# A distance-bias table spread over 128 partitions and recorded ahead of the q/k/v projection, and expert rows fetched by indirect DMA, in a two-block transformer kernel

## The chip, the cores and the metric

The kernel runs on one core of a Trainium2 chip. Its time is the device time of one execution in microseconds (us); the median of three runs stands for a kernel. TensorE (PE) does matrix products, its weight loads (PEld) run beside them; VectorE (DVE), ScalarE (ACT) and GpSimd (POOL) do the rest; SyncE (SP) only issues transfers. Sixteen DMA engines serve all transfers of the core.

## The reference

Two transformer blocks in a row on one sequence of 512 tokens of 1024 values, in float32. Two places of them matter here.

The first block's attention adds to each score a bias that depends only on the distance between query and key and on the head (32 buckets of distance, 8 heads):

```
def shared_bias(dist):
    return rel_bias[t5_bucket(dist)].transpose(2, 0, 1).reshape(G, R, *dist.shape)
...
s = jnp.einsum('bgrqd,bgkd->bgrqk', qc, kw) + shared_bias(dist)
p = masked_softmax(s, mask)
```

The second block ends in a mixture of experts: a router picks 2 of 32 experts for each token, and an expert is a gated pair of 1024x256 products and a 256x1024 product:

```
combine = jnp.sum(jax.nn.one_hot(e_idx, N_EXPERTS) * weights[..., None], axis=1)
for e in range(N_EXPERTS):
    act = jax.nn.silu(hf @ w_gate[e]) * (hf @ w_up[e])
    y = y + combine[:, e:e + 1] * (act @ w_down[e])
```

## The kernel before, in words

Everything lies on one core. Weights stream from DRAM in tiles of 128 partitions x 1024 values (512 KB), tokens are handled in four chunks of 128, and products of float32 are made exact enough by splitting operands into a high part and a rest (names ending in h and l).

**What sets the order.** The functions don't issue instructions: they record them in a plan, with tiles that belong to size classes (tags) of a fixed number of buffers; the class "t4" of 128x1024 tiles has 38, and holds streamed weights as well as kept tiles. `order()` (line 264) then runs a list scheduling: each engine, by a simple model of speeds, always takes the first recorded instruction that is ready, and a load may be taken ahead of its place where its class has a buffer to spare. `issue()` (line 400) issues them all, and so nearly every row of the trace names L409. Each engine runs its own list strictly in order. All ordinary transfers are issued by SP, in one list; when one of them must wait (for a buffer, or for the data that it stores), all behind it wait.

**The bias.** `bias_tables()` (line 830) builds a table R of 8 heads x 640 distances on 8 partitions: two products with a one-hot matrix, subtracted from a row of "far" values. One transfer then writes R to DRAM as `Rd`, 128 copies of each head's row (8 x 128 x 640 values, 2.62 MB), so that a read with a row step of 639 gives each query its shifted row. `bias(r)` (line 850) reads the shifted rows of two heads into tiles `B` (128x512 each) and copies from them on DVE the bias of the compressed keys (`cbias`). `nsa(r)` then makes the scores of those heads: PE (kT,qT), DVE (the row maximum `nst`), ACT (the exponential `P`). In `block1()` (line 1199) the order of recording is `qkv(0)` (queries), `compress_in()`, `qkv(1)` (keys, values), `bias_tables()`, the gates, `compress()`, and then the four rounds of `bias(r)` and `nsa(r)`.

**The experts.** `route_chunk` and `route` (lines 1638, 1681) give logits, the two experts of a token and its place (`place`) among the tokens of each expert. `rest_chunk` (line 1669) and `route_chunk` keep the normalised rows of all 512 tokens on the chip, split in a high part `xh` and a rest `xl` (eight t4 tiles). `experts()` (line 1794) goes over 16 pairs of experts; an expert has 64 slots, a pair fills 128 partitions. For each pair `gather()` (line 1777) compares `place` with the slot numbers on DVE (tile `oh`), and 16 products of 128x512 with `xh` and `xl` pick the rows of the slots; two copies (ACT and DVE) bring them to `X`. Then come 8 transposes (ident,X), 32 matmuls with the gate and up weights into H (8 tiles `wg` of 512 KB per pair), the activation, two transposes, 16 matmuls with the down weights (8 tiles `wd` of 256 KB), the scaling by the tokens' weights into `Y`, and an indirect DMA of POOL that adds the rows of Y to the output (`out_rows`) at the tokens given by `si`. `tables()` (line 1756) makes `si` and the slot weights `wt` behind pair 0. If an expert had more than 64 tokens, further rounds would follow.

Of the kernel before, what the change touches and what calls it, by code (L numbers as in the profile page):

```python
# [47 lines left out]
class View:  # L48
    """A part of a planned tile: a stand-in access pattern, and the steps to it from the whole tile."""
# [45 lines left out]
    def box(self):  # L95
        """partitions, range of elements and, where the tile has rows, range in a row."""
# [31 lines left out]
class Offset:  # L128
    """Row offsets of an indirect DMA."""
# [49 lines left out]
class Plan:  # L179
    """Records the instructions of a program in a plain order, then issues them in an order in which every  # L180
    engine, by a simple model of its speed, always takes the first recorded instruction that is ready.  A tile
    is taken ahead of the plain order only where its tag has a buffer to spare up to its place in it."""
# [24 lines left out]
    @contextmanager  # L207
    def together(self):
        """the instructions of the body, all on one engine, stay in one piece."""
        self.grouped = []  # L210
        yield
        g, self.grouped = self.grouped, None
        self.record([(g[0][0][0][0], [x[0][0][1:5] for x in g], None, None, None, sum(x[0][0][5] for x in g), None, False)],
                    [v for x in g for v in x[1]], [v for x in g for v in x[2]])

    def record(self, alts, writes, reads, load=False):
# [9 lines left out]
        for v in reads:  # L226
# [249 lines left out]
def price(self, eng, meth, args, kw):  # L476
    """Nanoseconds that an instruction holds its engine, roughly."""
# [30 lines left out]
class Net:  # L508
# [68 lines left out]
    def pair4(self, name):  # L577
        """four [128, 512] operands of split products."""
# [9 lines left out]
    def slab(self, src, name="w", scale=None):  # L588
        """[128, 1024] of weights: high part and rest; scale: factors of 512 columns."""
# [13 lines left out]
    def mm3(self, ps, pairs, byk=False):  # L603
        """ps = sum over (lhs hi, lhs lo, rhs hi, rhs lo)."""
# [11 lines left out]
    def rsqrt(self, v, n, scale, out=None):  # L616
        """v -> (v * scale + EPS) ** -0.5 on [p, n], in a new small tile or in out."""
# [25 lines left out]
    def constants(self):  # L643
# [11 lines left out]
        # the table of functions, ahead of the data  # L655
# [12 lines left out]
    def load_rows(self, src, name):  # L668
        """the four chunks of rows."""
# [5 lines left out]
    def norm_rows(self, x):  # L675
        """x * rstd, token major."""
# [8 lines left out]
    def new_hT(self, src=None):  # L685
        """hidden states, transposed and split; src: 32 more columns, multiplied on the way."""
# [62 lines left out]
    def scaled(self, out, ps):  # L749
        """out = ps / rms in the first block, ps in the second."""  # L750
# [36 lines left out]
    def narrow(self):  # L787
        """the 32 more columns, token major: psum [128, (chunk, 32)]."""
# [8 lines left out]
    def gemm_t(self, src, name="gt"):  # L797
        """columns on partitions: psum [128 cols, 512 tokens]."""
# [15 lines left out]
    def gemm_part(self, ps, grp, c, lhs_hi, lhs_lo, ks):  # L814
        """adds the products of k tiles ks to ps."""
# [6 lines left out]
    def gemm_r(self, grp, c, lhs_hi, lhs_lo, byk=False):  # L822
        """tokens on partitions: psum [128 tokens of chunk c, 512 cols]."""
# [6 lines left out]
    def bias_tables(self):  # L830
        nc, I = self.nc, self.I
        oh, R = self.t4("tab0")[:32, 0:640], self.t4("tab1")[:8, 0:640]
        nc.sync.dma_start(oh, I["oh"])
        rb = self.small([32, 8], "rb", bufs=1)
        nc.sync.dma_start(rb, I["rel_bias"])
        nc.sync.dma_start(R, I["far"].to_broadcast([8, 640]))
# [13 lines left out]
    def bias(self, r):  # L850
        """negated bias of the two heads of r, [query of a block, key], and that of the compressed keys."""
# [16 lines left out]
    def qkv(self, grp, acc=None, W=None):  # L868
        """q (grp 0) or the keys and values (grp 1): normalised, transposed; values token major."""
# [121 lines left out]
    def silu2(self, ps, name):  # L991
        """2 * silu of a psum tile."""
# [8 lines left out]
    def split_into(self, hi, lo, src, scale):  # L1001
        """hi + lo = src * scale."""
# [4 lines left out]
    def cmp_attention(self, r):  # L1007
        """weights over the compressed keys, times the gate, transposed: [(chunk % 2, g, key), (chunk // 2, query)]."""
# [73 lines left out]
    def lru_setup(self):  # L1082
# [7 lines left out]
        # softplus(-lambda)  # L1090
# [48 lines left out]
    def conv(self, up, wname, bname, i, nt):  # L1139
        """causal depthwise convolution along the tokens of a [128, 512] tile."""  # L1140
# [9 lines left out]
    def log1p(self, out, y, z, q):  # L1150
        """out = log1p(y) for y in [0, 1]; z, q scratch."""
# [10 lines left out]
    def gate_tile(self, wg, i):  # L1162
        """tanh(x / 2) of one tile of merge gates."""
# [8 lines left out]
    def merge(self, wg, g0, wp, a_hi, a_lo, b_hi, b_lo):  # L1172
        """sigmoid gates over two projections, split for the output product."""
# [82 lines left out]
            # sums over the partitions: four groups of 32 equal rows, 256 columns each  # L1256
# [29 lines left out]
    def conv_silu2(self, idx, i):  # L1286
        """2 * silu(conv(.)) of column tile idx."""
# [10 lines left out]
    def prefix(self, p, tri, ones, v, n):  # L1298
        """sums over the tokens up to each one; v [128, (chunk, n)]."""
# [6 lines left out]
    def mgates(self):  # L1306
        """per token and head: a = i - F, exp(-(F + M)); and the rows of M."""
# [83 lines left out]
    def rope_tables(self):  # L1391
        """cos and sin of position * inv_freq, [128, 4 chunks, 8]."""
# [33 lines left out]
    def qk_diff(self, grp, wname, scale, name):  # L1426
        """rms-normalised, rotated, transposed; one [128 = 2 maps x 64, 512] tile per head."""
# [36 lines left out]
    def diff(self, qT, kT, vd, after):  # L1464
        nc = self.nc
        # lam
# [64 lines left out]
    def block2(self):  # L1531
# [40 lines left out]
        for h in range(2):  # L1572
# [7 lines left out]
            for c in range(NCH):  # L1580
# [7 lines left out]
                if h and c:  # L1588
                    self.rest_chunk(c - 1)

# [1 line left out]
    def route_setup(self):  # L1592
        """router weights with the modulation in them, and what the shift adds to the logits."""
# [27 lines left out]
        # per token: its number, weights over the experts  # L1621
# [11 lines left out]
        self.X, self.XT, self.Y = [self.t4(n, keep=True) for n in ("X", "XT", "Y")]  # L1633
        self.x2T, self.sq2, self.gat = {}, {}, {}
        self.xh = [self.t4(f"xh{c}", dt=F32R, keep=True) for c in range(NCH)]
# [372 lines left out]
```

## Time and profile before

| | |
|---|---|
| runs (us) | 1160.14, 1158.07, 1157.68; median 1158.07 |
| span of the profiled execution | 1157.3 us |
| busy, share of the span | PE 1080.1 us (93%), DVE 653.8 (56%), ACT 405.3 (35%), POOL 189.7 (16%) |
| mean DMA rate | 188 GB/s |
| loads of expert weights | wg 128 x 512 KB, wd 128 x 256 KB |

The profile gives the span alone, from the first to the last instruction; the time that a run reports is 0.8 us above it in the median, and that difference is taken as what lies around the span. A share of busy time is an average over stages with different limits, so each stage is read by itself.

### The profile page before, as it was taken

To read this page: it belongs to the slowest core of one execution; us is meant where nothing else is said; L and a number is where in the kernel's file an instruction comes from. 1 tells how busy PE (TensorE), PEld (TensorE's weight loads), DVE (VectorE), ACT (ScalarE), POOL (GpSimd) and SP (SyncE) were. 2 spreads that over 40 slices of the span, in tenths; PEclk is the share of its full clock that TensorE was granted. 3 is DMA by queue.
4 is the path that set the end of the run, shared out by engine and by line. 5 is a ranking of instruction groups with operands and counts; after the bars stand their busy time and mean duration, and the time that the engine had idled before them with its cause. 6 is when DMAs were issued, how large, how long until landed. Compare 5 with 4: busy or idle time off the path is not lost.

```text
span 1157.3 us, 15019 instructions
## 1 busy us (share of the span) xinstructions
PE 1080.1 (93%) x5414; PEld 757.7 (65%) x5414; DVE 653.8 (56%) x1459; ACT 405.3 (35%) x824; POOL 189.7 (16%) x180
## 2 busy tenths in 40 slices
PE   7994299999999999999999999999999999999995
PEld 6773167777788777777677887788787444444431
DVE  4841288989656474776978786544717322333221
ACT  6320166756222243634663342222325111111120
POOL 2300033200111122420130201100204101111011
PEclk9996599999999999999999999999999999999998
DMA  9635810113443471815044322545966999999981
GB/s 346 227 88 87 247 46 20 37 56 95 131 143 119 163 255 53 296 37 220 10 158 157 129 86 73 178 131 156 354 264 219 349 387 363 371 385 367 389 292 26
DMA packets 74506, 217.22 MB, mean 188 GB/s; under 512 B 10820, under 2 KB 12428, under 8 KB 74424
## 3 DMA queue, kind: packets, MB, share of 16 engines
q1 hardware_dynamic: 72120, 211.98, 52.5%
q0 software_dynamic: 2304, 4.20, 2.1%
q8 instruction: 45, 0.74, 0.3%
q14 instruction: 37, 0.30, 0.1%
HBM read 204.56 MB, written 15.22 MB: 190 GB/s over the span
## 4 chain that ended last, share of the span: by engine, by line
PE 60%; DMA 14%; issue 11%; DVE 9%; SPq 2%; ACT 2%; another core or an unknown queue 1%; POOL 0%; POOLq 0%; DVEq 0%; ACTq 0%
PE b L409 59%; DMA out_rows<-Y,si 11%; SPq L409 2%; PE H L409 1%; DVE P L409 1%; DVE dP L409 1%; DMA gr<-in_wo 1%; DMA gr<-in_wa 1%; DMA B<-Rd 1%; DVE ada_acc L409 1%; ACT grh L409 1%; DVE grl L409 1%; DVE dq L409 0%; DVE uc L409 0%
## 5 line engine op out<-in xcount | busy, mean ns | idle before, releaser
L409 PE MATMUL b<-hTh,gth 128*128 128x512 f32 x464 | 124.5, 404 | 0.0
L409 PE MATMUL b<-hTh,gtl 128*128 128x512 f32 x464 | 121.1, 399 | 0.0
L409 PE MATMUL b<-hTl,gth 128*128 128x512 f32 x464 | 119.3, 395 | 0.0
L409 PE MATMUL H<-wg,XT 128*64 128x512 f32 x512 | 114.8, 596 | 0.0
L409 PEld LDWEIGHTS b<-hTh,gth 128*128 128x128 f32 x464 | 86.8, 190 | 22.2 <-issue 3.5
L409 PEld LDWEIGHTS b<-hTh,gtl 128*128 128x128 f32 x464 | 87.0, 189 | 20.5 <-issue 1.6
L409 PEld LDWEIGHTS b<-hTl,gth 128*128 128x128 f32 x464 | 86.4, 188 | 19.4 <-issue 0.9
L409 POOL TENSOR_TENSOR gtl<-gt,gth 128x1024 fp32r<-128x1024 f32 x23 | 56.4, 2455 | 247.0 <-ACT gth L409 222.4
L409 PEld LDWEIGHTS H<-wg,XT 128*64 128x64 f32 x512 | 35.0, 137 | 68.5 <-issue 59.5
L409 DVE SCALAR_TENSOR_TENSOR ada_acc<-ada_w,cols,ada_acc 128x1024 f32<-128x1024 f32 x42 | 60.3, 1435 | 7.5 <-DMA ada_w<-in_w_ada 7.5
L409 POOL DMA_INDIRECT out_rows<-Y,si x16 | 25.0, 1563 | 236.0 <-DVE Y L409 203.0
L409 PE MATMUL b<-grh,hTh 128*128 128x512 f32 x192 | 57.1, 410 | 6.0 <-ACT grh L409 6.0
L409 PE MATMUL b<-kT,qT 64*128 64x128 f32 (+3 forms) x128 | 26.4, 515 | 36.0 <-DVE nst L409 35.9
L409 PE MATMUL b<-wd,aT 128*64 128x512 f32 x256 | 58.4, 598 | 1.5 <-ACT aT L409 1.5
L409 ACT ACTIVATE gth<-gt 128x1024 fp32r<-128x1024 f32 x54 | 56.4, 1049 | 6.7 <-DMA gt<-in_wb 6.6
L409 DVE SCALAR_TENSOR_TENSOR act<-act,H 128x256 f32<-128x256 f32 x32 | 13.4, 420 | 79.6 <-ACT act L409 79.1
L409 PE MATMUL b<-grl,hTh 128*128 128x512 f32 x192 | 57.0, 405 | 0.0
L409 POOL TENSOR_TENSOR grl<-gr,grh 128x1024 fp32r<-128x1024 f32 x15 | 39.4, 2635 | 100.0 <-ACT grh L409 87.6
L409 ACT ACTIVATE P<-P,nst 128x128 f32<-128x128 f32 (+3 forms) x64 | 35.3, 553 | 57.2 <-DVE nst L409 57.0
L409 PE MATMUL b<-grh,hTl 128*128 128x512 f32 x192 | 55.3, 400 | 0.0
L409 DVE SCALAR_TENSOR_TENSOR Y<-b,wt,gate 128x512 f32<-128x512 f32 x32 | 24.0, 750 | 49.8 <-PE b L409 49.4
L409 DVE TENSOR_TENSOR gtl<-gt,gth 128x1024 fp32r<-128x1024 f32 x35 | 42.6, 1222 | 14.8 <-ACT gth L409 13.1
(380 smaller groups left out, 1973.6 us busy)
## 6 DMA issues: line engine op xcount, KB each, us to landing
wg<-in_wgu SPq DMA_DIRECT2D x128, 512.0 KB
wd<-in_wd SPq DMA_DIRECT2D x128, 256.0 KB
gt<-in_wb SPq DMA_DIRECT2D x58, 512.0 KB
ada_w<-in_w_ada SPq DMA_DIRECT2D x48, 512.0 KB
gr<-in_wa SPq DMA_DIRECT2D x23, 512.0 KB
wp<-in_wp SPq DMA_DIRECT2D x16, 512.0 KB
gr<-in_wo SPq DMA_DIRECT2D x16, 512.0 KB
cw<-in_cmp_w SPq DMA_DIRECT2D x8, 512.0 KB
```

The costliest lines, as they stand in the source:

```text
L409: i = getattr(getattr(self.nc, eng), meth)(*[val(a) for a in args], **{k: val(v) for k, v in kw.items()})
```

## The change

**The bias table.** The 32x8 table is spread on chip to 32x128 (each head 16 times), so that one product with the one-hot matrix gives the table on 128 partitions, 16 equal ones for each head; POOL writes the constant of the last 128 columns, and the input "far" goes. `Rd` has the same contents and the same bytes, but is now written from 128 partitions, each of which gives 8 copies. `bias_tables()` is recorded ahead of `qkv(0)`.

**The experts.** `route_chunk` stores the normalised rows of each chunk, unsplit, in a DRAM tile `x2d` (512x1024, 2.1 MB in all). `route` now also makes the slot numbers as it goes (`sl`, and products of `sl` with the token numbers in `slp`), and `slots()` turns them into `si` before pair 0. `fetch(i)` is an indirect DMA of POOL that reads the 128 rows of pair i from `x2d` straight into one of two buffers X; `fetch(0)` stands ahead of the loop and `fetch(i + 1)` at the top of pair i. `rest_chunk`, `gather`, the tiles `xh` and `xl` and the two copies to X are gone; `weights()` takes over the making of `wt`. The rest of the pairs is as before. The diff also drops comments.

```diff
 def bias_tables(self):
-        oh, R = self.t4("tab0")[:32, 0:640], self.t4("tab1")[:8, 0:640]
+        oh, R = self.t4("tab0")[:32, 0:512], self.t4("tab1")[:, 0:640]
...
-        for a, b in ((0, 512), (512, 640)):
-            p = self.pst()
-            nc.tensor.matmul(p[:8, :b - a], rb, oh[:, a:b], start=True, stop=True)
-            nc.vector.scalar_tensor_tensor(R[:, a:b], p[:8, :b - a], -1.0, R[:, a:b], op0=OP.mult, op1=OP.add)
+        rx = self.sq128("rx")[:32, :]
+        nc.vector.tensor_copy(rx.rearrange("p (h i) -> p h i", i=16), rb.unsqueeze(2).to_broadcast([32, 8, 16]))
+        p = self.pst()
+        nc.tensor.matmul(p, rx, oh, start=True, stop=True)
+        nc.gpsimd.memset(R[:, 512:640], BIG)
+        nc.vector.tensor_scalar(R[:, 0:512], p, -1.0, None, op0=OP.mult)
...
-        nc.sync.dma_start(Rd, R.unsqueeze(1).to_broadcast([8, 128, 640]))
+        nc.sync.dma_start(Rd.rearrange("h (i r) m -> (h i) r m", r=8), R.unsqueeze(1).to_broadcast([128, 8, 640]))
...
 def block1(self):
-        self.qkv(0, self.hT_first())
+        acc = self.hT_first()
+        self.bias_tables()
+        self.qkv(0, acc)
         self.compress_in()
         self.qkv(1, W=self.group(I["wa1"][1]))
-        self.bias_tables()
...
 def route_chunk(self, c, h, x):
-        nc.scalar.activation(self.xh[c], x, AF.Copy, scale=r)
+        xn = self.t4("x2n")
+        nc.scalar.activation(xn, x, AF.Copy, scale=r)
+        nc.sync.dma_start(self.x2d[c * 128:(c + 1) * 128, :], xn)
...
 def route(self, lo, hi):
+        for c in range(lo, hi):
+            nc.vector.tensor_tensor(self.sl[:, c].rearrange("p k (a b) -> p k a b", a=2),
+                                    self.io.unsqueeze(1).unsqueeze(1).to_broadcast([128, 2, 2, 64]),
+                                    self.pos[:, c].unsqueeze(2).unsqueeze(3).to_broadcast([128, 2, 2, 64]), op=OP.is_equal)
+            for k in range(2):
+                nc.tensor.matmul(self.slp[:, :32], self.sl[:, c, k], self.tw[:, c, k, 0:32], start=c + k == 0,
+                                 stop=c == NCH - 1 and k == 1)
...
+    def fetch(self, i):
+        self.nc.gpsimd.indirect_dma_start(out=self.X[i % 2], out_offset=None, in_=self.x2d,
+                                          in_offset=Offset(self.si[:, i:i + 1]), bounds_check=511, oob_is_err=False)
...
 def experts(self, first=False):
+        self.fetch(0)
         for i in range(16):
-            ps = self.gather(i, NCH - 1 if first and i < 2 else 0)
-            nc.scalar.activation(X[:, :512], ps[0], AF.Copy)
-            nc.vector.tensor_copy(X[:, 512:], ps[1])
+            X = self.X[i % 2]
+            if i < 15:
+                self.fetch(i + 1)
```

The planner moves instructions on every engine. Three places follow, in rows of each engine's list (destination, sources, size; the numbers behind a name are those of the tile).

SP's list in the first block, where the table is written. Before, behind the weights of the gates (gt) and of the modulation (ada_w):

```order
L409 DMA gt<-in_wb 128x1024 x2
L409 DMA ada_w<-in_w_ada 128x1024
L409 DMA gt<-in_wb 128x1024
L409 DMA Rd<-tab_276 1024x1x640
L409 DMA gt<-in_wb 128x1024
L409 DMA ada_w<-in_w_ada 128x1024
L409 DMA gt<-in_wb 128x1024 x2
L409 DMA ada_w<-in_w_ada 128x1024
L409 DMA gt<-in_wb 128x1024 x2
L409 DMA B_766<-Rd 128x512
L409 DMA B_779<-Rd 128x512
```

With the change, among the weights of the compression (cw) and the stores that shift its keys (kcS):

```order
L409 DMA wd<-in_wd 128x512
L409 DMA cw_335<-in_cmp_w 128x1024
L409 DMA cw_355<-in_cmp_w 128x1024
L409 DMA wd<-in_wd 128x512
L409 DMA Rd<-tab_78 1024x1x640
L409 DMA cw_406<-in_cmp_w 128x1024
L409 DMA kcS<-kcT 64x512 x2
L409 DMA cw_440<-in_cmp_w 128x1024
L409 DMA cw_469<-in_cmp_w 128x1024
L409 DMA kcS<-kcT 64x512 x2
L409 DMA B_518<-Rd 128x512
L409 DMA B_533<-Rd 128x512
```

The write moved from row 41 of SP's list to row 30, and the first reads from row 47 to row 36; the loads of gt that stood between them now stand behind the reads.

PE's list in two consecutive pairs of experts. Before, the 16 products of a gather are mixed among the matmuls of the pair ahead:

```order
L409 MATMUL b<-ident,X 128x128 x8
L409 MATMUL b<-xh_7313,oh 128x512 x2
L409 MATMUL H<-wg,XT 64x512 x16
L409 MATMUL b<-xl_7332,oh 128x512 x2
L409 MATMUL b<-xh_7372,oh 128x512 x2
L409 MATMUL b<-xl_7425,oh 128x512 x2
L409 MATMUL b<-xh_7470,oh 128x512 x2
L409 MATMUL b<-ident,act 128x128 x2
L409 MATMUL b<-xl_7497,oh 128x512 x2
L409 MATMUL b<-xh_7265,oh 128x512 x2
L409 MATMUL b<-wd,aT 64x512 x8
```

With the change only the pair's own matmuls and transposes are left:

```order
L409 MATMUL H<-wg,XT 64x512 x12
L409 MATMUL b<-ident,X_6898 128x128 x8
L409 MATMUL H<-wg,XT 64x512 x2
L409 MATMUL b<-ident,act 128x128 x2
L409 MATMUL H<-wg,XT 64x512 x2
L409 MATMUL b<-wd,aT 64x512 x8
L409 MATMUL H<-wg,XT 64x512 x12
L409 MATMUL b<-ident,X_6900 128x128 x8
L409 MATMUL b<-ident,X_6898 128x128 x4
```

The transposes of the next pair now stand among the H matmuls of the pair ahead, and read X straight from the fetch.

SP's list where the experts begin (xr are the rows of the residual, stored to the output chunk by chunk). Before:

```order
L409 DMA wg<-in_wgu 128x1024 x12
L409 DMA wd<-in_wd 128x512
L409 DMA out_rows<-xr_6453 128x1024
L409 DMA wd<-in_wd 128x512
L409 DMA out_rows<-xr_6457 128x1024
L409 DMA wd<-in_wd 128x512
L409 DMA out_rows<-xr_6460 128x1024
L409 DMA wg<-in_wgu 128x1024 x6
L409 DMA wd<-in_wd 128x512
L409 DMA out_rows<-xr_6463 128x1024
L409 DMA wd<-in_wd 128x512 x3
L409 DMA wg<-in_wgu 128x1024 x7
```

With the change:

```order
L409 DMA wg<-in_wgu 128x1024 x22
L409 DMA wd<-in_wd 128x512
L409 DMA out_rows<-xr_6452 128x1024
L409 DMA x2d<-x2n 128x1024
L409 DMA wd<-in_wd 128x512
L409 DMA out_rows<-xr_6456 128x1024
L409 DMA wd<-in_wd 128x512
L409 DMA out_rows<-xr_6459 128x1024
L409 DMA wg<-in_wgu 128x1024 x3
L409 DMA x2d<-x2n 128x1024
L409 DMA wg<-in_wgu 128x1024
L409 DMA x2d<-x2n 128x1024
```

More loads of wg stand ahead of the last chunk's store, since eight t4 tiles (xh, xl) are free; the stores of x2d stand among them.

## Rows read from the trace of the kernel before

**Rows 1.** The page: granted clock and DMA share in 40 slices of 28.9 us.

```profile
PEclk9996599999999999999999999999999999999998
DMA  9635810113443471815044322545966999999981
```

**Rows 2.** Timeline of PE: start, busy us, engine, line, instructions, [idle before <- releaser].

```profile
99.18 2.00 PE L409 MATMUL b<-hTh,gtl 128*128 128x512 f32 x8
137.08 1.43 PE L409 MATMUL b<-kT,qT 64*128 64x256 f32 x4 [35.91 <-DVE nst L409]
```

**Rows 3.** Waits from 85 to 145 us: engine, waited for, us, times, longest.

```profile
PE b L409 <- DVE nst L409: 35.9, 1, 35.9
DVE cbias L409 <- DMA B<-Rd: 44.1, 1, 44.1
SPq L409 <- DMA Rd<-tab: 6.1, 1, 6.1
```

**Rows 4.** Timeline of SP's queue, parts from 34 to 60 and from 72 to 128 us.

```profile
41.48 1.18 SPq L409 DMA_DIRECT2D kcS<-kcT  x2
...
72.90 0.82 SPq L409 DMA_DIRECT2D Rd<-tab  x1
...
126.84 0.33 SPq L409 DMA_DIRECT2D B<-Rd  x1
```

**Rows 5.** Windows: stretch, us, busy (count) of PE, PEld, DVE, ACT, POOL, clock, DMA, GB/s.

```profile
36.00:73.00 37.00, 35.60 (x166) 28.18 (x166) 26.04 (x49) 7.49 (x16) 4.82 (x2) 1.00 0.45 152
73.00:127.00 54.00, 26.41 (x151) 18.71 (x147) 10.54 (x29) 4.05 (x8) 3.46 (x4) 0.72 0.56 86
848.00:896.00 48.00, 45.89 (x258) 37.38 (x258) 21.48 (x83) 18.84 (x35) 15.36 (x25) 1.00 0.74 279
896.00:1122.00 226.00, 225.01 (x1060) 101.22 (x1056) 70.79 (x151) 40.20 (x98) 20.71 (x14) 1.00 1.01 370
```

**Rows 6.** PE's groups from 896 to 1122 us: busy, mean ns, idle before.

```profile
L409 PE MATMUL H<-wg,XT 128*64 128x512 f32 x454 | 102.1, 596 | 0.0
L409 PE MATMUL b<-xh,oh 128*128 128x512 f32 x112 | 38.4, 414 | 0.0
L409 PE MATMUL b<-xl,oh 128*128 128x512 f32 x112 | 37.7, 416 | 0.0
L409 PE MATMUL b<-ident,X 128*128 128x128 f32 x120 | 16.3, 277 | 0.5 <-ACT X L409 0.5
```

**Rows 7.** Timeline of PE over the last two pairs.

```profile
1120.20 7.04 PE L409 MATMUL H<-wg,XT 128*64 128x512 f32 x32
...
1133.03 7.04 PE L409 MATMUL H<-wg,XT 128*64 128x512 f32 x32
```

**Rows 8.** Waits of SP's queue from 896 to 1122 us.

```profile
SPq L409 <- DMA wg<-in_wgu: 92.7, 88, 3.4
SPq L409 <- DMA wd<-in_wd: 32.1, 82, 1.6
SPq L409 <- PE H L409: 19.4, 24, 11.8
```

**Rows 9.** DMA queues from 896 to 1122 us: packets, MB, share of 16 engines.

```profile
q1 hardware_dynamic: 29497, 80.19, 93.1%
q0 software_dynamic: 1872, 3.20, 7.5%
```

**Rows 10.** The scatters of Y (tile Y): ns min/median/max, first and last start; landing.

```profile
L409 POOL DMA_INDIRECT out_rows<-Y,si x16: 1536/1544/1808, 909.7 to 1147.5; - x16
DMA to landing us min/median/max: 5.5/8.4/9.8
```

**Rows 11.** Timeline from 889 to 912 us, where the experts begin.

```profile
890.34 0.18 DVE L409 SCALAR_TENSOR_TENSOR place<-b,mk 128x32 f32<-128x32 f32 x1
...
892.93 1.03 PE L409 MATMUL b<-ident,X 128*128 128x128 f32 x8
...
896.49 5.46 SPq L409 DMA_DIRECT2D wg<-in_wgu  x7
```

More of the change, by code (lines that the diff above doesn't have):

```diff
@@ L1632, in route_setup @@
         self.wt = self.const("wt", [128, 16])
-        self.X, self.XT, self.Y = [self.t4(n, keep=True) for n in ("X", "XT", "Y")]
-        self.x2T, self.sq2, self.gat = {}, {}, {}
-        self.xh = [self.t4(f"xh{c}", dt=F32R, keep=True) for c in range(NCH)]
-        self.xl = [self.t4(f"xl{c}", dt=F32R, keep=True) for c in range(NCH)]
+        self.x2T, self.sq2 = {}, {}
+        self.x2d = self.tile("dram", [512, 1024], F32, "x2d", True)
     def route_chunk(self, c, h, x):
@@ L1726, in route, with slots @@
                                        mk[:, lo:hi], op0=OP.add, op1=OP.mult)
+        w = self.c1k("w32", s2)
+        nc.vector.tensor_tensor(w, oh, self.at[:, lo:hi].unsqueeze(2).to_broadcast(s2), op=OP.mult)
+        nc.vector.tensor_reduce(self.pos[:, lo:hi], w, axis=AX.X, op=OP.add)
+        nc.vector.tensor_tensor(self.tw[:, lo:hi, :, 0:32], oh,
+                                self.tok[:, lo:hi].unsqueeze(2).unsqueeze(3).to_broadcast(s2), op=OP.mult)
+        if lo == 0:
+            self.sl = self.t4("sl", (128, NCH, 2, 128))
+            self.slp = self.pst()
+        for c in range(lo, hi):
[5 more added lines that the diff above has]
+                                 stop=c == NCH - 1 and k == 1)
+    def slots(self, p):
+        nc = self.nc
+        u = self.small([128, 16], "tabu", bufs=1)
+        for e in range(2):
+            s = slice(64 * e, 64 * e + 64)
+            t = p[s, 16 * e:16 * e + 16]
+            nc.vector.tensor_scalar(u[s], t, 0.0, self.dummy[s], op0=OP.is_equal, op1=OP.mult)
+            nc.vector.scalar_tensor_tensor(self.si[s], t, -1.0, u[s], op0=OP.add, op1=OP.add)
     def weights(self):
@@ L1741, in weights @@
         nc.vector.tensor_tensor(st[:, 7], st[:, 6], st[:, 4], op=OP.mult)
-        t5 = lambda v, s: v.unsqueeze(2).unsqueeze(3).to_broadcast(s)
         s2 = [128, NCH, 2, 32]
-        nc.vector.tensor_tensor(self.tw[:, :, :, 0:32], oh, t5(self.tok, s2), op=OP.mult)
         nc.vector.tensor_tensor(self.tw[:, :, :, 32:64], oh,
                                 st[:, 6:8].rearrange("p k c -> p c k").unsqueeze(3).to_broadcast(s2), op=OP.mult)
-        w = self.c1k("w32", s2)
-        nc.vector.tensor_tensor(w, oh, self.at.unsqueeze(2).to_broadcast(s2), op=OP.mult)
-        nc.vector.tensor_reduce(self.pos, w, axis=AX.X, op=OP.add)
+        p = self.pst()
+        for c in range(NCH):
+            for k in range(2):
+                nc.tensor.matmul(p[:, :32], self.sl[:, c, k], self.tw[:, c, k, 32:64], start=c + k == 0,
+                                 stop=c == NCH - 1 and k == 1)
+        for e in range(2):
+            s = slice(64 * e, 64 * e + 64)
+            nc.vector.tensor_copy(self.wt[s], p[s, 16 * e:16 * e + 16])
         p = self.pst()
@@ L1767, in tables @@
                                  stop=c == NCH - 1 and k == 1)
-        t = self.small([128, 16], "tab", bufs=1)
+        self.slots(p)
         for e in range(2):
             s = slice(64 * e, 64 * e + 64)
-            nc.vector.tensor_copy(t[s], p[s, 16 * e:16 * e + 16])
             nc.vector.tensor_copy(self.wt[s], p[s, 32 + 16 * e:48 + 16 * e])
-        u = self.small([128, 16], "tabu", bufs=1)
-        nc.vector.tensor_scalar(u, t, 0.0, self.dummy, op0=OP.is_equal, op1=OP.mult)
-        nc.vector.scalar_tensor_tensor(self.si, t, -1.0, u, op0=OP.add, op1=OP.add)
-    def gather(self, i, lo=0, hi=NCH):
-        nc = self.nc
-        if lo == 0:
-            self.gat[i] = self.vm("oh", [128, NCH, 2, 64], F32R), [self.pmm(), self.pmm()]
-        oh, ps = self.gat[i]
-        s = [128, hi - lo, 2, 64]
-        nc.vector.tensor_tensor(oh[:, lo:hi], self.io.unsqueeze(1).unsqueeze(1).to_broadcast(s),
-                                self.at[:, lo:hi].rearrange("p c (e n) -> p c e n", e=2)[:, :, :, i].unsqueeze(3)
-                                .to_broadcast(s), op=OP.is_equal)
-        for c in range(lo, hi):
-            for k, x in enumerate((self.xh[c], self.xl[c])):
-                for h in range(2):
-                    nc.tensor.matmul(ps[h], oh[:, c].rearrange("p e n -> p (e n)"), x[:, h * 512:(h + 1) * 512],
-                                     start=c + k == 0, stop=c == NCH - 1 and k == 1)
-        return ps
+    def fetch(self, i):
+        self.nc.gpsimd.indirect_dma_start(out=self.X[i % 2], out_offset=None, in_=self.x2d,
+                                          in_offset=Offset(self.si[:, i:i + 1]), bounds_check=511, oob_is_err=False)
     def experts(self, first=False):
@@ L1797, in experts @@
         A, sh, G2 = self.mod[4], self.mod[3], self.mod[5]
-        X, y = self.X, self.Y
+        y = self.Y
         if not first:
@@ L1862, in moe @@
         nc = self.nc
+        self.X = [self.t4(f"X{k}", keep=True) for k in range(2)]
+        self.XT, self.Y = self.t4("XT", keep=True), self.t4("Y", keep=True)
+        for X in self.X:
+            nc.gpsimd.memset(X, 0.0)
         parts = (0, 2, 3, 4)
@@ L1865, in moe @@
             self.route(lo, hi)
-        self.rest_chunk(NCH - 1)
-        for lo, hi in zip(parts, parts[1:]):
-            for i in range(2):
-                if hi < NCH:
-                    self.gather(i, lo, hi)
+        self.slots(self.slp)
         self.experts(True)
@@ L1984, in layout @@
     d["rows"] = np.concatenate([rows[k].reshape(-1) for k in ROWS])[None, :]
-    dist = 511 - np.arange(640)
-    oh = np.zeros((32, 640), np.float32)
-    for m in range(512):
-        oh[_bucket(dist)[m], m] = 1.0
+    oh = np.zeros((32, 512), np.float32)
+    oh[_bucket(511 - np.arange(512)), np.arange(512)] = 1.0
     d["oh"] = oh
-    d["far"] = np.where(dist < 0, np.float32(BIG), np.float32(0)).astype(np.float32)[None, :]
     return {k: np.ascontiguousarray(v) for k, v in d.items()}
```

16 lines of the change are left out of this document (1 added, 15 removed).

## The prediction

> **What bounds the kernel now.** The page's slices are read first. The granted clock is at full speed nearly everywhere, with one hole in the slices from 87 to 145 us, and the DMA share is 0.9 or more in the expert stage at the end [rows 1]. So two stretches are looked at closely; the change touches both.
>
> The hole: PE ends a product at 101.2 us and starts the next at 137.1, and the 35.9 us between are the longest wait of that stretch [rows 2, 3]. PE waits for a row maximum of DVE, but DVE itself stood 44.1 us at `cbias` for the first tile B to land [rows 3]. SP explains B: the write of Rd was issued at 72.9 us, the first B only at 126.84, after SP had waited 6.1 us for just that write [rows 3, 4]. Rd thus took 53.9 us for 2.62 MB, 48.6 GB/s, while the window over that time has the engines 0.56 busy and only 86 GB/s in all [rows 5]. The source sits on 8 partitions. From B's issue to PE's start are 10.2 us more.
>
> The experts, 896 to 1122 us: PE is busy 225.0 of 226 us, which looks like the bound, but DMA is at share 1.01 and 370 GB/s in the same window [rows 5]. SP's own waits tell which is first: 92.7 + 32.1 = 125 us for its own loads to make headway, against 19.4 us for PE to free a tile [rows 8]. Both limits nearly touch here: work taken from PE alone is worth little until the last load has landed. What follows that load is another matter: from 1122 to 1157.3, 35.3 us, PE works off pairs whose weights are there already.
>
> **The bias table.** Before the reads of Rd there were its two small products and the store; now one product of 128x512 (about 0.4 us), two small DVE operations and one on POOL, all at about 35 us where PE is at the projection of q and DVE has 11 of 37 us free [rows 5]: nothing on the path beyond 0.5 us. In SP's list the write now stands just ahead of the stores kcS, which went out at 41.48 us [rows 4], and the table's inputs are there long before; I put it at 37 us, 36 earlier than before. How long it takes from 128 partitions no row shows. Lower bound: the same bytes at the rate of the expert stage, 370 GB/s [rows 5], are 7.1 us; upper bound: the old 53.9 us. It is nearest to the ordinary 128-partition transfers of the former, and beside other traffic at share 0.45 [rows 5] I take 7.1 / 0.55 = 13 us: landed at 50. With the 10.2 us behind B's issue, and a few for SP's list, the first scores could start by about 65, and PE comes to them at 101. So the wait of 35.9 us closes with some 35 us to spare, and even the upper bound would land Rd at 91 and let PE start at 101. What is late next: the loads of gt that stand behind the reads in SP's list; they now wait for Rd to 50, when before they waited behind the jam of the slow write. The end of the hole also spares PE a few us at half clock (the slices read 6 and 5 there [rows 1]), which I use against small new waits. Term: −36, bounds −40 and, if the write is as slow as before and holds SP's list to 91 us, −11 (below).
>
> [...]
>
> **The experts.** Removed from each pair: 8 + 8 gather matmuls. In the window the two groups took 38.4 + 37.7 = 76.1 us [rows 6], over 14 pairs some 5.4 us of span each (their busy times overlap a little), and the last two pairs, which have no gather, show what is left: 1133.03 − 1120.20 = 12.8 us from H to H [rows 7], 13.9 with the transposes of X (16.3 us for 15 groups of 8 [rows 6]). Two copies to X fall away on ACT and DVE, off the path once the gather is. Were PE the only limit, 16 pairs would now take about 222 us. They can't, since the weights don't come faster:
>
> *Length of the DMA phase.* In 226 us 83.6 MB were moved [rows 5]. By the lists the kernel before had 27 wg and 24 wd tiles issued before PE freed the first; with the change it is 34 and 24 (the eight tiles of xh and xl are weights now): 7 x 0.524 = 3.7 MB less to come, −9.9 us. Added are 15 fetches. Empty slots lie out of bounds and, as in the scatters, move nothing: 1024 rows of 4 KB in all, 3.9 MB of them in the phase. Priced as ordinary bytes that is +10.6 us; priced as the scatters (7.5% of the engines for 3.20 MB, against 93.1% for 80.19 MB [rows 9], twice as much a byte) +21. I take +11, since the scatters read and write and the fetch only copies: net +1, bounds 0 and +12. The 2.1 MB of x2d go out in the stretch before, whose share is 0.74 [rows 5]: its 12 us of idle engines take 2.1 / 370 = 5.7 us.
>
> [...]
>
> *Start of the phase.* It starts when PE frees the first wg. Before: the last `place` at 890.34, gather, copies, transposes at 892.93, first freed tile 896.49 [rows 11]. After: 890.5 + about 1.2 us for a few DVE steps of the kind of `place` (0.18 us, on larger tiles here; an estimate), about 1.4 for two small matmuls and the four DVE steps of slots(), fetch issue 1.5 and landing 8.4 as in the scatters [rows 10], then transposes as before: X at 903 in place of 892.9, +10; some us come back because POOL no longer makes xl in that stretch. I take +7, bounds 0 (a fetch on idle engines lands in much less) and +14.
>
> *Tail.* When weights are the limit, the last pair ends a fixed time behind its last loads. The last 8 wd (2.1 MB, 5.7 us at 370 GB/s) come behind the last wg. From the last quarter of H (1133.03 + 0.75 x 7.04 = 1138.3) to the end are 19.0 us [rows 7]. So the end is 19.0 − 5.7 = 13.3 us after the last byte, in place of 35.3: −22, bounds −22 and −15. A PE at 13.9 us a pair would be done some 10 us ahead of that, so it is not the limit, but not by much.
>
> **Sum**, on the profiled span: 1157.3 − 36 (hole) + 7 (start) + 1 (phase) − 22 (tail) = 1107.3. The runs' median lies 0.8 above the span: 1108. So 36 of the 50 us are the table's, and the larger edit, which takes 16 of the 64 wide matmuls out of each pair, brings 14.
>
> **Rivals.** A, the sum: 1108, own range 1100 to 1117.
>
> B, the experts give nothing: the first fetch at +14, the fetches at the scatters' price +12, tail −15: 1157.3 − 36 + 14 + 12 − 15 + 0.8 = 1133; between A and that 1117 to 1133. For it: a saturated window [rows 9]; against it: the start has idle engines.
>
> C, the wait moves: the write stays slow or SP's list jams at B, and the loads of gt behind it come from 91 us on; PE then lacks some 6 tiles, 3.1 MB, which take 11 to 21 us at the 279 to 152 GB/s of ordinary stretches [rows 5]: 1119 to 1129. For it: strictly ordered SP; against: the 370 GB/s that 128-partition transfers reach.
>
> D, the experts gain more: the rate rises, or the phase starts no later, and PE sets 13.9 us a pair: about 894.5 (behind the transposes at 892.93 [rows 11]) + 15 x 13.9 + 24 for the last (1157.3 − 1133.03 [rows 7]) = 1127, less the 36, plus 0.8: 1092; 1085 to 1100.
>
> E, the other side: the fetches are not hidden. POOL runs in order and its scatter waits for Y; if each fetch waited for the pair ahead, a pair would be 1.5 + 8.4 [rows 10] + 2.5 for transposes and XT + 12.8 [rows 7] = 25.2 us, 16 of them 403 in place of 264 (from the first transposes at 892.93 [rows 11] to the end): 1157.3 − 36 + 139 + 0.8 = 1261. It decides from (264 + 36) / 16 = 18.8 us a pair. Against it: two buffers X, the fetch a pair ahead, landing 9.8 at most beside 14 us of a pair.
>
> **Chances.** A 0.56, B 0.17, C 0.12, D 0.09, E 0.06. The forecast is A's. The range 1097 to 1133 holds A, B, C and a fifth of D, together 0.87, of which a little may spill over either end. About 0.2% (2.3 us) is what a measurement of this kernel can tell from no change. Only E is slower; were B and C to fall together, 0.01 would lie near no change: faster 0.93, same 0.01, slower 0.06.
>
> **What would show it.** Right: no wait of more than 5 us on PE between 95 and 140 us, Rd landed before 65 us, the first B long before PE wants it; in the experts no xh and xl, H to H about 14.2 us, DMA share still about 1.0, PE with 0.5 to 1 us waits for weights in each pair, the last wd landing 13 us before the end. Wrong: PE waiting for DVE or gt near 90 to 110 us (C); transposes waiting for X in each pair (E); first H after 905 − 36 (B); the DMA share below 0.95 with PE full (D).

## The result and the profile after

The changed kernel takes 1127.08 us in the median of four runs (1124.24 to 1128.45), the kernel before 1159.11 (1157.68 to 1161.48); the ratio is 0.9714, interval 0.9696 to 0.9731. The profiled execution of the change has a span of 1122.5 us and a time of 1124.24, the lowest of its four. The forecast was 1108: the sign and the range (1097 to 1133) held, but of 50 us expected only 32 came, and the sum's own range (A, 1100 to 1117) did not hold the result; that of rival B (1117 to 1133) did.

The hole in PE's work is gone, and the page's slices show it (28.1 us each; granted clock and DMA share, as in [rows 1]):

```profile
PEclk9999989999999999999999999999996999999998
DMA  9981100224345717160232433446699899999995
```

The clock reads 9 in the first 30 slices but for an 8 in the sixth, and DMA reads 9 from the 30th slice (814 us) to the last but one, with one 8. The 6 in the 31st slice (842 to 870 us) is new; it comes back below. SP's timeline shows the table (compare [rows 4]):

```profile
36.71 0.64 SPq L409 DMA_DIRECT2D Rd<-tab  x1
...
50.06 2.03 SPq L409 DMA_DIRECT2D B<-Rd  x4
...
85.66 18.23 SPq L409 DMA_DIRECT2D B<-Rd  x2
103.94 0.42 SPq L409 DMA_DIRECT2D gt<-in_wb  x1
106.26 25.25 SPq L409 DMA_DIRECT2D B<-Rd  x2
```

The write goes out at 36.71 us and the reads at 50.06; among SP's waits between them (for DVE and PE) is none for the write, so it had landed by then. The trace's packet records give its own time: 1024 packets of 2560 bytes in both kernels, from 74.4 to 126.5 us before, and from 38.0 to 45.9 us now. The waits from 85 to 145 us answer to [rows 3]:

```profile
PE b L409 <- DVE kbd L409: 1.8, 1, 1.8
...
DVE cbias L409 <- DMA B<-Rd: 0.5, 1, 0.5
```

35.9 us of PE's wait became 1.8 on something else, and DVE's 44.1 us became 0.5.

In the experts the windows (columns as in [rows 5]) now read, in three stretches: ahead of the first freed weight tile, from there to the last byte of the loads, and the tail:

```profile
860.00:872.00 12.00, 4.08 (x14) 2.34 (x16) 1.78 (x7) 1.50 (x4) 3.28 (x3) 0.50 1.01 395
872.00:1106.00 234.00, 202.50 (x900) 69.94 (x896) 58.98 (x127) 36.80 (x89) 37.06 (x28) 0.99 0.99 359
1106.00:1122.00 16.00, 4.16 (x17) 1.27 (x16) 1.50 (x2) 0.38 (x1) 1.56 (x1) 0.78 0.24 45
```

For the kernel before the middle stretch, cut in the same way, is:

```profile
898.00:1121.00 223.00, 222.01 (x1044) 100.28 (x1042) 69.19 (x148) 39.75 (x97) 20.37 (x13) 1.00 1.02 374
```

PE was busy 222 of 223 us and is now busy 202.5 of 234: over the whole stretch it is no longer the limit. The loads are, and they became slower, 359 GB/s in place of 374. What SP waits for says the same (872 to 1106 us, as [rows 8]):

```profile
SPq L409 <- DMA wg<-in_wgu: 88.8, 81, 3.3
SPq L409 <- DMA wd<-in_wd: 40.4, 81, 2.1
SPq L409 <- PE H L409: 16.6, 10, 9.8
SPq L409 <- PE b L409: 13.2, 12, 5.0
```

The first 38 us of the stretch differ from the rest: PE is full there, the engines are at 0.93, and nearly all of SP's waits for PE end in them (27.9 of 29.8 us; the longest, 9.8, begins before 872). First the windows, then the waits from 872 to 910 us:

```profile
872.00:910.00 38.00, 37.66 (x184) 13.75 (x182) 10.54 (x24) 7.34 (x19) 6.29 (x5) 0.99 0.93 323
910.00:1106.00 196.00, 164.84 (x720) 56.19 (x715) 48.44 (x103) 29.46 (x70) 30.77 (x23) 0.99 1.00 366
```

```profile
SPq L409 <- PE H L409: 15.9, 7, 9.8
SPq L409 <- PE b L409: 12.0, 8, 5.0
```

Four landmarks give the balance of the two spans (the last logits are where DVE reads them; the loads end where their rate falls, known to about 2 us):

| from | to | before, us | after, us | difference | predicted |
|---|---|---|---|---|---|
| start | last router logits | 883.35 | 851.10 | −32.3 | −36 |
| last logits | first H product | 11.2 | 18.7 | +7.5 | +7 |
| first H product | end of the loads | 226.5 | 236.2 | +9.7 | +1 |
| end of the loads | end | 36.3 | 16.5 | −19.8 | −22 |
| whole span | | 1157.3 | 1122.5 | −34.8 | −50 |

So the step that was off most is the length of the load phase; the hole gave 3.7 us less than its size. The spans differ by 34.8 us and the medians by 32.0, since the profiled execution of the change is its fastest, 2.8 us below the median.

### The profile page after: what moved, and what is told of

The parts are those of the page before. It is cut to its first block, busy times and chain, and to the rows that moved or that the text cites. A ratio compares the mean times of both kernels' runs of the same rounds, so it can differ in the third digit from the quotient of the medians.

```text
span 1122.5 us, 14439 instructions
## 1 busy us (share of the span) xinstructions
PE 1042.7 (93%) x5172; PEld 722.4 (64%) x5172; DVE 637.7 (57%) x1432; ACT 393.3 (35%) x803; POOL 187.4 (17%) x173
## 5 line engine op out<-in xcount | busy, mean ns | idle before, releaser
L409 PE MATMUL H<-wg,XT 128*64 128x512 f32 x512 | 128.6, 606 | 10.7 <-DMA wg<-in_wgu 7.7
L409 PEld LDWEIGHTS H<-wg,XT 128*64 128x64 f32 x512 | 38.1, 138 | 86.3 <-issue 51.9
L409 DVE SCALAR_TENSOR_TENSOR ada_acc<-ada_w,cols,ada_acc 128x1024 f32<-128x1024 f32 x42 | 64.7, 1540 | 7.2 <-DMA ada_w<-in_w_ada 7.1
L409 PE MATMUL b<-wd,aT 128*64 128x512 f32 x256 | 61.7, 613 | 7.3 <-ACT aT L409 4.3
L409 DVE TENSOR_SCALAR XT<-b,mod,mod 128x128 f32<-128x128 f32 x64 | 24.2, 407 | 76.7 <-PE H L409 67.2
L409 ACT ACTIVATE XT<-b,mod,mod 128x128 f32<-128x128 f32 x64 | 27.3, 456 | 88.8 <-PE H L409 71.6
L409 ACT ACTIVATE grh<-gr 128x1024 fp32r<-128x1024 f32 (+1 forms) x39 | 39.9, 1036 | 31.0 <-DVE gr L409 9.4
L409 DVE SCALAR_TENSOR_TENSOR mg<-mg,b 128x512 f32<-128x512 f32 x32 | 21.9, 685 | 43.6 <-PE b L409 43.4
```

The costliest lines, as they stand in the source:

```text
L409: i = getattr(getattr(self.nc, eng), meth)(*[val(a) for a in args], **{k: val(v) for k, v in kw.items()})
```

## The experiments

Twelve kernels were run. Five theories were held against each other, on two questions. **P**: the table's gain is the spread over partitions; **O**: it is the place in the order. **L**: with the fetches in, the transfers set the end of the experts; **S**: the late first X does; **G**: the experts' part is worth a good part of the gain by itself. All times are medians; the kernel before, run beside them, took 1159 to 1160 us.

### Each part alone

`t_only` puts the new `bias_tables()` and its early recording into the kernel before:

```diff
-        self.qkv(0, self.hT_first())
+        acc = self.hT_first()
+        self.bias_tables()          # on 128 partitions
+        self.qkv(0, acc)
```

> Table part of the change alone, experts as before. Theory L (in the experts the transfers set the end, so work taken from PE there pays little): the table is worth nearly the whole result, 1124 to 1129 us. Rival G (the split of the prediction, scaled: about a quarter of the gain is the experts'): 1133 to 1138 us. Both expect the wait of 35.9 us on PE to be gone.

Measured: 1127.86 us, ratio 0.9727 (0.9699 to 0.9756). `x_only` is the changed kernel with the old table at the old place.

> Expert part of the change alone, table as before. Theory L: within 5 us of the kernel before, 1153 to 1159 us, with the last load landing some 16 us before the end in place of 36 and the phase of the loads longer. Rival G: 1145 to 1150 us.

Measured: 1157.31 us, ratio 0.9985 (0.9970 to 1.0001). The table is nearly the whole result; the expert part gives some 2 us, with an interval that touches zero. G falls.

### Spread or order

`t128_late` spreads the table and leaves it where it was recorded; `t8_early` moves the old one ahead.

```diff
 # t128_late, against the kernel before, in words
-        Rd write from 8 partitions
+        Rd write from 128 partitions
 # t8_early, against the kernel before, in words
-        self.bias_tables()          # behind qkv(1)
+        self.bias_tables()          # ahead of qkv(0)
```

> Table on 128 partitions, recorded at the old place; experts as before. Theory P (the 8 source partitions make the write slow, and nothing else is wrong with it): the write issued at about 73 us lands before 90, the wait on PE falls from 36 us to under 5, 1124 to 1132 us. Rival O (the place in the order is what was missing): the wait stays above 20 us, 1143 to 1158 us.

Measured: 1116.99 us, ratio 0.9617 (0.9590 to 0.9643), 10 us below the change itself and 7 below what P expected. SP's timeline:

```profile
72.15 0.62 SPq L409 DMA_DIRECT2D Rd<-tab  x1
...
81.65 2.92 SPq L409 DMA_DIRECT2D B<-Rd  x2
```

The write leaves as late as before, at 72.15 us, and 9.5 us later the reads go out, after a wait of 1.5 us for it: 53.9 us became 9.5. The packets themselves run from 73.4 to 81.3 us. In the change, with the same 1024 packets in the same 7.9 us, about 15 are under way at a time and one takes 118 ns in the mean, where before there were at most 8 and one took 375 ns. PE has no wait above 1.8 us from 85 to 145 us. That is P, and O falls.

> Table on 8 partitions as before, recorded ahead of the q projection; experts as before. Theory P: the write still takes about 50 us, from 37 to about 88, the loads issued in that time crawl, and PE waits for them or for B: 10 to 25 us of the gain are missing, 1133 to 1148 us. Rival O: the early start alone hides the write, 1124 to 1130 us.

Measured: 1161.2 us, ratio 1.001 (0.9995 to 1.0026): all of the gain is missing, more than P expected. SP's timeline shows why:

```profile
35.11 0.82 SPq L409 DMA_DIRECT2D Rd<-tab  x1
36.04 23.29 SPq L409 DMA_DIRECT2D cw<-in_cmp_w  x2
59.42 9.45 SPq L409 DMA_DIRECT2D kcS<-kcT  x2
68.97 9.36 SPq L409 DMA_DIRECT2D cw<-in_cmp_w  x2
78.42 12.08 SPq L409 DMA_DIRECT2D kcS<-kcT  x2
91.30 3.15 SPq L409 DMA_DIRECT2D B<-Rd  x4
```

Two loads of 512 KB took 23.3 us to issue behind the slow write, and the stores kcS, the first of which left at 41.48 us before [rows 4], went out from 59.42 us on. DVE stood 42.5 us for them, and PE 26.1 us ahead of the compression's first product (waits from 30 to 130 us; the profile names no releaser for PE's):

```profile
DVE blk L409 <- DMA kcS<-kcT: 42.8, 2, 42.5
...
PE H L409 <- issue: 26.1, 1, 26.1
```

The wait was moved, not removed: the write from 8 partitions held up the transfers issued behind it, and early in the program they are needed at once. It had done so at its old place too, as one load of the kernel before shows:

```profile
79.31 18.16 SPq L409 DMA_DIRECT2D ada_w<-in_w_ada  x1
```

### Why the early table is slower than the late one

`t128_mid` records the spread table between `compress_in()` and `qkv(1)`. `t_b_late` is `t_only` with the reads of B held back:

```diff
             B = self.a2(f"B{h}")
+            nc.vector.tensor_copy(B[:, 0:1], self.kT[1][:, 0:1])
             nc.sync.dma_start(B, ...)
```

> Table alone, spread, recorded between the compression's inputs and the keys and values: behind the q projection, ahead of the old place. If what costs 11 us in the early recording is that the table stands ahead of the q projection and the compression: 1115 to 1120 us, as at the old place. If it is the order that follows once Rd is there before the gates (the same rows of SP's list from the reads of B on): 1124 to 1130 us.

> Table alone, spread and recorded early, but the reads of B held until the keys are there at about 78 us (a copy of one column from them into each B first). If the early reads, which take buffers and SP's list from the gate weights, are why the early recording is 11 us slower than the late one: 1116 to 1120 us. If the cause is another part of the plan: 1125 to 1130 us.

Measured: `t128_mid` 1126.97 us (ratio 0.9729, 0.9705 to 0.9752), `t_b_late` 1125.21 us (0.9703, 0.9684 to 0.9721). Standing ahead of the q projection isn't the cost, and the early reads are at most 2.7 us of it. The windows of `t_only`, and then of `t128_late`, show where part of it lies:

```profile
85.00:200.00 115.00, 106.42 (x796) 77.66 (x795) 95.87 (x333) 68.41 (x197) 29.82 (x27) 0.97 0.10 31
200.00:250.00 50.00, 48.28 (x195) 36.21 (x194) 39.55 (x53) 29.70 (x37) 2.45 (x1) 1.00 0.26 77
```

```profile
85.00:200.00 115.00, 109.23 (x803) 79.40 (x802) 95.34 (x351) 70.26 (x196) 31.33 (x30) 0.94 0.22 81
200.00:250.00 50.00, 49.94 (x203) 37.70 (x203) 42.73 (x59) 30.55 (x39) 2.25 (x2) 1.00 0.29 87
```

With the early table PE works 154.7 us of 165, with the late one 159.2, in the same stretch: 4.5 us less, beside half the transfers in its first part. In the timeline of the change above SP stands for 18.23 and 25.25 us at reads of B, with one load of gate weights between them; with the late table it issues several first. That this is the cause isn't shown. By the last logits the gap between the two kernels is 6.8 us (849.1 against 842.3), by the end 10.2. Another 3.4 us of it are the down products, 61.8 us for all 256 in `t_only` against 58.4: the granted clock was 0.73 from 1096 to 1102 us, where some of its last ones ran. What sets the rest wasn't found: all orders with the table ready before the gates took 1125 to 1128 us, the two with it at the old place and without mixing gathers and fetches 1117 to 1118.

### The experts' part

`x_t128late` is the whole change with the table at its old place:

> The whole change, but with the table recorded at its old place, behind the keys and values. Theory L with P (the spread source is the gain, the early recording costs some 10 us, the experts' part gives 0 to 3): 1114 to 1118 us. Rival G (the experts' part is worth more once the table is out of the way): below 1110. A third way, that the 10 us of the early recording come from an accident of that one plan: 1122 to 1128.

Measured: 1117.54 us, ratio 0.9623 (0.9588 to 0.9659); with the experts as before it was 1116.99. The experts' part gives nothing in this order either.

`no_fetch` leaves out what the fetches of pairs 2 to 15 bring:

```diff
-            if i < 15:
+            if i < 1:
                 self.fetch(i + 1)
```

> The changed kernel without the fetches of pairs 2 to 15, which compute with the rows of pairs 0 and 1 instead: this part of the computation is left out. Theory L (the transfers set the end): 3.7 MB less at 359 GB/s, 10 us faster than the changed kernel, 1115 to 1119 us, first H of pair 0 at the same time. Theory S (the late first X is what costs, the fetches behind it are hidden): within 3 us, 1124 to 1130.

Measured: 1109.67 us, 17.4 below the change, and 5 below what L expected. POOL's queue moved 3.72 MB less (4.68 in place of 8.40). About 3 us of the difference lie ahead of the experts (last logits at 847.9 in place of 851.1). In the load phase SP's first load behind a freed tile left at 870.43 and the loads ended at 1090, some 220 us where the change has 234. So leaving out 3.72 MB saved about 13 to 14 us, 3.6 us per MB. That is more than the DMA engines spent on them. The queues (packets, MB, share of 16 engines) of the kernel before from 898 to 1121 us, of the change from 872 to 1106, and of `no_fetch` from 868 to 1090:

```profile
q1 hardware_dynamic: 29398, 79.96, 94.0%
q0 software_dynamic: 1872, 3.20, 7.6%
```

```profile
q1 hardware_dynamic: 28385, 76.34, 86.0%
q0 software_dynamic: 4161, 7.51, 12.7%
```

```profile
q1 hardware_dynamic: 28535, 76.71, 90.9%
q0 software_dynamic: 2160, 3.81, 8.9%
```

Share times window over bytes gives 2.6 us of all 16 engines per MB for ordinary loads, 5.3 for the scatters (the kernel before), and for the fetches (29.7 − 19.8) / 3.70 = 2.7, the price of ordinary bytes. The other 4 us that `no_fetch` saved are engines that were less busy.

`hold8` takes eight t4 tiles out of use, as xh and xl did:

```diff
+        self.held = [self.t4(f"held{k}", keep=True) for k in range(8)]
+        for t in self.held:
+            nc.gpsimd.memset(t[:, 0:8], 0.0)
```

> The changed kernel with eight t4 tiles held and not used through the experts, as xh and xl held them before: 8 loads of wg fewer can go ahead. Theory L: 4.2 MB more to come behind the first freed tile, 6 to 11 us slower, 1133 to 1138 us. Theory S: within 3 us, 1124 to 1130.

Measured: 1139.28 us, 12.2 above the change (ratio to the kernel before 0.9814, 0.9764 to 0.9864), 1 above what L expected. Its loads end at about 1119 us, 13 later than in the change. `w_late` makes the token weights wait for the slot numbers:

```diff
+        nc.vector.scalar_tensor_tensor(st[:, 6], self.u[:, 0:4], 0.0, st[:, 6], op0=OP.mult, op1=OP.add)
         nc.vector.tensor_tensor(st[:, 7], st[:, 6], st[:, 4], op=OP.mult)
```

> The changed kernel with the slot weights held back until the slot numbers are made, so that 8 small products leave the way of the first fetch: the first X about 2.5 us earlier. Theory S: 2 to 3 us faster, 1123 to 1126 us. Theory L: under 1.5 us, 1125 to 1128.

Measured: 1126.11 us (1122.84 to 1128.58), 1.0 below the change, inside its spread. In the change the slot numbers wait for small products of which eight are not theirs; the timeline:

```profile
854.62 0.18 DVE L409 SCALAR_TENSOR_TENSOR place<-b,mk 128x32 f32<-128x32 f32 x1
...
855.46 4.48 PE L409 MATMUL b<-tw,sl 128*128 128x32 f32 x20 [0.90 <-DVE tw L409]
...
860.17 0.18 DVE L409 SCALAR_TENSOR_TENSOR si<-b,tabu 64x16 int32<-64x16 f32 x1
...
860.65 1.29 POOL L409 DMA_INDIRECT X<-x2d,si  x1 [10.36 <-DMA wd<-in_wd]
...
867.92 1.94 PE L409 MATMUL b<-ident,X 128*128 128x128 f32 x8 [7.98 <-DMA X<-x2d,si]
```

In `w_late` the numbers are there 3 us earlier, 2 of them by the edit, since the last logits are already 1.0 us earlier (850.1 in place of 851.1); the fetch leaves only 1 us earlier:

```profile
856.91 0.38 DVE L409 SCALAR_TENSOR_TENSOR si<-b,tabu 64x16 int32<-64x16 f32 x2
859.67 1.29 POOL L409 DMA_INDIRECT X<-x2d,si  x1 [10.35 <-DMA wd<-in_wd]
```

What it waits for next is a transfer. The profile names a load of wd that it doesn't need; it does need the last store of x2d, issued at 851.50 us in the change and queued with the loads, so that is the likelier one. The first H came 1.0 us earlier, no more than the logits: the edit didn't move the start, so this run says nothing for or against S. `no_fetch` and `hold8` speak for L: their first H came 2.2 us earlier and 2.8 later than in the change, of 17.4 and 12.2 us, so the start of pair 0 explains a small part of either.

### A mixture that should have been better

With the late table and the experts as before, PE is the limit and the loads end at about 1078 us, 38 ahead of the end; with all rows fetched the loads are the limit. So a few fetched pairs at the end looked best. `hyb3` keeps the gathers for 13 pairs and fetches the last three, `hyb5` the last five:

```diff
+            if k0 <= i + 1 < 16:        # k0 = 13 or 11
+                self.fetch(i + 1)
+            if i < k0:
                 ps = self.gather(i, NCH - 1 if first and i < 2 else 0)
```

> The spread table at its old place, and the gathers on PE kept for 13 pairs of experts; only the last three pairs fetch their rows by indirect DMA. If the two limits of the expert stage stand side by side (theory L): PE loses 3 x 5.4 = 16 us of the 38 us that it needs behind the last load in the run with the table alone at its old place, the loads land 5 to 10 us later for the rows stored and fetched, and the end comes 16 us behind them: 1102 to 1109 us, faster than every kernel so far. If the fetches cost as much as they save at any number: 1114 to 1119 us.

> The same with five fetched pairs. Theory L: PE is no longer the limit, the loads land another 2 us later than with three: 1104 to 1111 us, not faster than with three. If PE is still the limit at three: 1096 to 1102 us.

Measured: 1122.32 us (1119.42 to 1126.33; ratio 0.9694, 0.9665 to 0.9723) and 1123.19 (1115.18 to 1125.79; 0.9667, 0.9630 to 0.9704): both medians are slower than no fetch at all. The expectation took a gather out at its full 5.4 us. PE's timeline of the last pairs of `hyb3` shows what is left:

```profile
1065.34 7.04 PE L409 MATMUL H<-wg,XT 128*64 128x512 f32 x32
1073.86 0.41 PE L409 MATMUL b<-ident,act 128*128 128x128 f32 x2 [1.48 <-DVE act L409]
1074.74 3.65 PE L409 MATMUL b<-wd,aT 128*64 128x512 f32 x16 [0.47 <-ACT aT L409]
1078.23 7.04 PE L409 MATMUL H<-wg,XT 128*64 128x512 f32 x32
1086.66 0.44 PE L409 MATMUL b<-ident,act 128*128 128x128 f32 x2 [1.39 <-DVE act L409]
1087.57 5.35 PE L409 MATMUL b<-wd,aT 128*64 128x512 f32 x16 [0.47 <-ACT aT L409]
```

A pair without a gather waits 1.5 + 0.5 us for DVE and ACT in its own chain, time which gather products of the next pair had filled, and some of its down products take 5.35 us in place of 3.65. H to H is 12.9 and 14.5 us here. The loads ended at 1089 us, 11 later than without fetches. And the start moved, which the expectation left out. The first H, in `t128_late` and then in `hyb3`:

```profile
853.01 7.09 PE L409 MATMUL H<-wg,XT 128*64 128x512 f32 x32
```

```profile
859.46 7.09 PE L409 MATMUL H<-wg,XT 128*64 128x512 f32 x32
```

The products that make the slot numbers stand ahead of pair 0 there, where `t128_late` has most of them behind its first H: 6.4 us later, of which 0.7 were there at the last logits. From the first H to the end `hyb3` took 258 us in place of 263. So the three fetched pairs gave 5 us in place of 16, and the start took that back. In `hyb5` the last logits themselves came 6 us later (848.3) and the first H at 867.92.

## Why the prediction was right and where it was wrong

**The hole, −36: the cause right, the term 3.7 us too large.** The write from 8 partitions was the cause, and the wait of 35.9 us closed entirely. The 13 us taken for the new write were more than the 7.9 that its packets took. From 8 partitions they took 52.1, a factor of 6.6 for a sixteenth of the partitions, with at most 8 under way at a time in place of about 15; by what means the partitions set the rate, no run shows. What the prediction didn't see is that the early recording, which it counted as a free 36 us of head start, changes the order that follows. At the old place the same table gives 43 us (41.0 at the last logits, more than the term's bound of 40). Its sentence that the wait closes "with some 35 us to spare" held the point without drawing it: the move wasn't needed. The remark that even the old write would only cost part of the gain (bound −11) was wrong: `t8_early` gave nothing, because the loads for the compression stand behind it.

**The start, +7: right, with some luck in the size.** First H came 7.5 us later, for the reason given, but two errors offset each other: the slot numbers came 5.7 us behind the last `place` where 2.6 were put down, and the rows 7.3 us behind the fetch where 9.9 were. The lower bound of 0 took a fetch on idle engines to land in much less; in the change the engines were at share 1.01 from 860 to 868 us, while the first fetch was under way, so this was not shown. Two things were not in the sum. The slot numbers shared PE with products for the weights, which `w_late` shows to have cost the numbers 2 us and the first H nothing. And the granted clock was 0.51 from 852 to 862 us and 0.50 from 862 to 872 (half clock), where PE was busy 5.8 and 4.1 of 10 us: the 20 small products took 4.48 us, and H of the first pair 8.49 where the later ones take 7.04.

**The load phase, +1: the step that failed.** It grew by 9.7 us, and by 11 from window to window (223 to 234 us). The bytes were right, 84.0 MB against 83.3. The queues' shares give the parts as time of all 16 engines. The weights gave 8.4 us for the 9.9 credited, and `hold8`, which loses 12.2 us, shows that the credit was real. The fetches took 9.9 us for the 11 put down, so their price as ordinary bytes was right too. What failed is what the sum put at nothing. The phase now ends nearer the end of the work, and 15 scatters fall into it in place of 13: +2.9 us. And the engines were less busy, 0.99 in place of 1.02, which is the remaining 6.6 us. About half of that (0.09 of 38 us, 3.4) lies in the first 38 us, at 0.93, where SP waited some 19 us for PE to free tiles (27.9 without the part of the longest wait that lies ahead): the prediction had the loads as the limit from the first freed tile on, but PE, starting late, was the limit until it had caught up. The cause of the other half isn't shown. Without any fetch (`no_fetch`) the phase still took 220 us, 3 less than before, where the credit alone was 9.9. The upper bound of +12 held the phase.

**The tail, −22: right** to 2 us; the end follows the end of the loads by 16.5 us in place of 36.3. (The 0.8 us added for what lies around the span was 1 us short: in the runs of the change a time lies 1.7 to 1.8 us above its own span.)

**The split between the parts was wrong.** The prediction gave the table 36 and the experts 14 of 50 us. The runs with one part alone give 32 and 2. The three terms of the experts nearly cancel: 19.8 gained at the tail, 7.5 lost at the start and 9.7 in the phase. Rival B (the experts give nothing, 1117 to 1133) is what happened, and its sign, the first H after 905 − 36 = 869 us, was met at 869.79. Its terms had the right direction at about two thirds of their size together: start +7.5 for its +14, phase +9.7 for its +12. Its reason for the phase, fetches at the scatters' price, was wrong (2.7 us of engine time per MB, not 5.3). The phase's term priced the fetches as time taken from the loads, though POOL issues them and SP the loads. The trace bears that out: the shares of the two queues add to 99% in the change (86.0 and 12.7), and leaving the fetches out made the phase 13 to 14 us shorter.

## What to carry to other kernels

The table's write from 8 partitions was a double fault: it was slow (52.1 us of packets, against 7.9 from 128 partitions), and it held up what was issued behind it (two loads of 512 KB took 23.3 us to issue in `t8_early`). So move such a write only once it is spread, and then see whether moving it still pays; here it didn't (`t_only` 1127.86 us, `t128_late` 1116.99). Where two limits stand side by side, as PE and the loads do here, work shifted from one to the other paid only until the other was reached (the experts' part alone gave some 2 us); its price there must be measured, and `no_fetch`, one line left out, does it; the shares of the queues then tell bytes from idle engines. In a program whose order comes from a planner, every edit is also a new order: a change and its placement are two experiments.

## What was not expected of the hardware

In `hyb3` a short wait of PE was followed by a spell at half clock in one pair and not in the pair before: the same 16 products, behind the same waits of about 1.4 and 0.5 us, took 5.35 us in the one (granted clock 1.00 from 1084 to 1086 us, 0.50 from 1088 to 1090) and 3.65 in the other. Single runs of the two mixtures differ by 7 and 11 us, those of the kernel before by up to 6. And rows fetched by an indirect DMA landed evenly, 6.7 to 7.5 us after issue, with the engines full, where the scatters took 6.7 to 9.1:

```profile
L409 POOL DMA_INDIRECT X<-x2d,si x16: 984/1033/1292, 860.7 to 995.8; - x16
...
DMA to landing us min/median/max: 6.7/7.3/7.5
```
